# Gates' projection in seven half products with weight sets through a ring of three, and sums of halves of h on GpSimd

## The chip, the cores and the metric

One core of a Trainium2 chip. Its engines are named PE (TensorE's matmuls; PEld its weight loads), DVE (VectorE), ACT (ScalarE), POOL (GpSimd) and SP (SyncE, which here only issues DMAs). The metric is the device time of one execution in microseconds, the median of the runs.

## The reference, cut to what matters

One layer of a hybrid decoder on 4096 tokens of width 1024, in float32. All groups read one input h and come from one projection; each is multiplied by its own SiLU gate.

```
shift, scale, gate = jnp.split(c_act @ ada_w + ada_b, 3, axis=-1)
h = _rmsnorm(x, g_pre) * (1.0 + scale[:, None]) + shift[:, None]
proj = h @ w_in
aq, ak, av, ag, rkv, rg, gq, gkk, gv, gg = jnp.split(proj, ...)
attn = _sliding_window_attention(aq, ak, av, sinks) * jax.nn.silu(ag)
rwkv = _rwkv7_mixer(h, rr, rk, rv, ...) * jax.nn.silu(rg)
gla = _gla_mixer(h, gq, gkk, gv, ...) * jax.nn.silu(gg)
y = jnp.concatenate([attn, rwkv, gla], axis=-1) @ w_out
return x + gate[:, None] * _rmsnorm(y, g_post)
```

The gates' projection is the part of h @ w_in that gives ag, rg and gg: 1024 by 1024 weights for each token.

## The kernel before, in words

The tokens are cut into 16 pieces of 256 (NS = 16, NT = 256). Every large product is made of three matmuls in f16: each operand is split in a high and a low f16 part, and high x high, high x low and low x high are summed in PSUM.

*First half* (to about 980 us). For each piece, h is made and kept in DRAM (hscr), and the two recurrent mixers run; their results go to DRAM (mscr). In stage_c (line 949), which goes along with the pieces, the weights that the second half needs are read in f32, scaled, split in f16 parts and written to DRAM: seven sets of 256 columns of w_in (wscr), and the output weights. Those are cut in four quarters, and group (918) makes from the quarters the seven operands of a product by half blocks, with GpSimd for the differences (tile cs), ACT and VectorE for the splits (tile ch), into woscr.

*Second half*. One trip for each piece i (stage_p2, 1970): the output projection of piece i-1 (outp), the gates of piece i, and the projection of q, k and v for piece i+1 (qkv, heads_of). Beside these run the attention of a piece (stage_s, attend) and stage_m (1791), which multiplies the mixers' results (tiles mxa, mxb) by the gates (tile ag), finds a scale from their sum of squares (the small product mp, then tiles mtot to msc), and splits sums and differences of their halves into four f16 blocks (tile mtp, block at 1769).

- gates_of (1675): four products of 256 columns, tile gp, two PSUM banks (pj) in turn for all of gp, qp, kp and op. Weights q3 to q6 stay in SBUF for the whole half. Each product is two times 24 matmuls with 256 tokens moving, and is read twice: ACT's tanh and VectorE's multiplication. Two buffers of ag serve in turn, so gates(i) waits for the use of ag by piece i-2 ("og").
- outp (1867): seven products of a half block (tile op), 12 matmuls of 512 columns each. Weights of four products stay in SBUF (tiles o), three go through one buffer (ov), whose halves SP loads again when they have been used. VectorE adds each product to tile yv.
- heads_of (1625): kp (24 matmuls), two products qp (48 each), vp (48 of 128 columns). kp is read by ACT and VectorE into kT, two times two instructions each; qp into q.
- attend (1700): scores sc = q x k in eight groups of matmuls, read by a VectorE instruction with a maximum (CUSTOM in the profile), exponentials on ACT, the product with v (ovp).

The order is not that of the code. Every instruction is noted with a modelled cost (Order.note, 100), and pin (225) lays the instructions of each engine in a fixed row; an instruction of the row waits for its semaphores, and those behind it wait with it. PE, DVE, ACT, POOL and SP each have one such row.

All calls go through one helper, so in the profile nearly every instruction has line L339; the names of tiles tell them apart.

Of the kernel before, what the change touches and what calls it, by code (L numbers as in the profile page):

```python
# [35 lines left out]
URGENT = 150  # L36
HOME = {('kp', 'mq'): 'tr', ('cw', 'm'): 'at'}
# [366 lines left out]
def hybrid_kernel(ctx, tc, x, xc, rows, ada1, adaw, w1, wl, w2, wo, cst, abias, out):  # L404
# [45 lines left out]
    wscr = dp.tile([7, P, 2, KD * 256], F16, name="wscr")  # L450
# [180 lines left out]
    w_inv = [cp.tile([P, 1], F32, name=f"winv{n}") for n in range(8)]  # L631
    wo_ss = cp.tile([P, 2 * KD], F32, name="wo_ss")
    wo_sc = cp.tile([P, 1], F32, name="wo_sc")
    g_h = [cp.tile([P, 1], F32, name=f"gh{n}") for n in range(4)]
# [9 lines left out]
    with ExitStack() as p1:  # L644
# [264 lines left out]
        def wo_squares(h):  # L909

            for j in range(8 * h, 8 * h + 8):
                s32 = piece(wo, j * 512)
                yield [s32]
                square(s32, wo_ss[:, j : j + 1])
            if h:
                yield from total(wo_ss, wo_sc, w_inv[7])

        def group(k, c):

            left, right = [wt([P, 512], "cs", 2).rearrange("p (h n) -> p h n", h=2) for _ in range(2)]  # L920
            for t, k8 in ((left, k), (right, 4 + k)):
                for h in range(2):
                    at = (c + 2 * h) * 2048 + k8 * 256
                    SP.dma_start(t[:, h], wo[:, at : at + 256])
# [3 lines left out]
            def parts(t, p, m):  # L928
# [3 lines left out]
                S.activation(z[:, :, 0, :], t, AF.Identity, scale=wo_sc)  # L932
                V.scalar_tensor_tensor(z[:, :, 1, :], t, wo_sc, z[:, :, 0, :], op0=ALU.mult, op1=ALU.subtract)
                for n in range(m):
                    to = woscr[p + n, :, k, 2 * c : 2 * c + 2]
# [13 lines left out]
        def stage_c(i):  # L949

            yield [("c", i - 1), ("vg", i)]
            for n in ((0,), (1, 2), (3,), (4, 5), (6,))[i] if i < 5 else ():
# [31 lines left out]
                if n > 2:  # L984
                    V.tensor_single_scalar(g_h[n - 3], inv, 0.5, op=ALU.mult)
            if 4 <= i < 6:
                yield from wo_squares(i - 4)
            elif 6 <= i < NS - 2:
                yield from group((i - 6) % 4, (i - 6) // 4)
# [557 lines left out]
    def pool2(name):  # L1547
# [3 lines left out]
        "q", "kT", "vt", "w5", "w6", "ab", "v4", "pr", "pT", "mxa", "ag", "mtp", "mxb", "sm1", "o1", "o6", "o4", "o5", "ov")}  # L1551
# [8 lines left out]
    Wq = []  # L1560
# [6 lines left out]
    def stage_w(_):  # L1567

        load_h(0)
        order = (2, 0, 1, 3, 4, 5, 6)  # L1570
        got = {}
        for n in order:
            slot = wslot if n < 5 else lambda name: pools[f"w{name[1]}"].tile([P, KD, 256], F16, name=name)
            got[n] = load_2(n, slot(f"q{n}h"), slot(f"q{n}l"))
            if n == 1:
                load_h(1)
        Wq.extend(got[n] for n in range(7))
# [89 lines left out]

    def gates(i):
        yield [("og", i - 2)]
        f = F[i]  # L1670
        f["ag"] = ag = t_A([P, 8, NT], "ag") if i == 0 else pools["ag"].tile([P, 8, NT], F32, name="ag2") if i == 1 else F[i - 2]["ag"]
        yield from gates_of(f["hT"], ag, pjt)
        done.add(("gates", i))

    def gates_of(hT, ag, pj):

        for n in range(4):
            yield ["pj"]
            gp_ = pj("gp")
            for b in range(2):  # L1680
                yield from proj(gp_[:, b * NT : (b + 1) * NT], Wq[3 + n], b * P, P, hT)
            av = ag[:, 2 * n : 2 * n + 2, :].rearrange("p b n -> p (b n)")
            model.order.urgent = URGENT
            S.activation(av, gp_, AF.Tanh, scale=g_h[n])
            V.scalar_tensor_tensor(av, av, 1.0, gp_, op0=ALU.add, op1=ALU.mult)
            model.order.urgent = 0
# [91 lines left out]
    def mix_scale(mss):  # L1778
# [9 lines left out]
        V.tensor_mul(oi, miv, w_inv[7])  # L1788
        return msc, oi

    def stage_m(i):
# [45 lines left out]

    def load_o(t, n):
# [360 lines left out]
```

## Time and profile before

| | |
|---|---|
| median of 3 runs | 1996.33 us (1994.67 to 1996.79) |
| the profiled execution's own time | 1996.2 us |
| its span, first to last instruction | 1994.4 us |
| mean granted TensorE clock | 0.991 |
| busy: PE, PEld, DVE | 1882.8, 1453.4, 1427.5 us |
| busy: ACT, POOL | 1115.0, 373.1 us |
| DMA, mean | 129 GB/s |

A row of busy time counts what an engine executes; PE's matmuls overlap, so the time from one matmul's start to the next one's says more of the pace than the duration of one. In the rows of a tile, the three numbers are the shortest, the median and the longest duration in ns. In a timeline, the bracket at the end says how long the engine had been idle and for whom it waited.

### The profile page before, as it was taken

The numbers are of one execution on the slowest core, as the hardware profiler recorded it, in microseconds if no ns is written. First come the engines' busy times: TensorE is split into PE (matmuls) and PEld (weight loads), VectorE is DVE, ScalarE is ACT, GpSimd is POOL, SyncE is SP. The second block draws the span as 40 slices with busy tenths as digits, with TensorE's granted clock in tenths as the row PEclk, the third lists the DMA queues.
The fourth block names the chain that finished last, engine by engine and source line by source line (L and its number), as shares of the span: only waits on it lengthen the run. The fifth ranks groups of instructions, "written<-read, shape, count | busy, mean of one in ns | idle before, by whom it ended". The sixth has DMA issues, their size and how long they took to land.

```text
span 1994.4 us, 59065 instructions
## 1 busy us (share of the span) xinstructions
PE 1882.8 (94%) x24651; PEld 1453.4 (73%) x24651; DVE 1427.5 (72%) x3919; ACT 1115.0 (56%) x2529; POOL 373.1 (19%) x549
## 2 busy tenths in 40 slices
PE   5799989999999999999999999999999999999997
PEld 1677777777777777777776677876778767787793
DVE  4877877788877888777647776667666676666766
ACT  4877878677786676565435443344434444434443
POOL 0623223543223454223200000000000000000001
PEclk8999999999999999999999999999999999999999
DMA  9345544443342433125234433344333443334315
GB/s 373 128 152 179 155 140 125 148 139 109 105 133 88 125 111 111 61 65 185 77 132 142 151 109 112 109 146 130 109 110 109 149 130 109 100 117 151 110 47 181
DMA packets 154261, 257.55 MB, mean 129 GB/s; under 512 B 49026, under 2 KB 100994, under 8 KB 147844
## 3 DMA queue, kind: packets, MB, share of 16 engines
q1 hardware_dynamic: 153844, 253.19, 39.7%
q8 instruction: 195, 3.19, 0.7%
q14 instruction: 78, 0.64, 0.1%
q10 hardware_dynamic: 144, 0.52, 0.1%
HBM read 192.83 MB, written 60.82 MB: 127 GB/s over the span
## 4 chain that ended last, share of the span: by engine, by line
PE 55%; DVE 23%; DMA 9%; ACT 6%; issue 4%; POOL 1%; SPq 1%; ACTq 0%; DVEq 0%; POOLq 0%
PE gp L339 16%; PE op L339 11%; PE qp L339 5%; PE zz L339 4%; PE pv L339 2%; PE kp L339 2%; PE ovp L339 2%; PE lp L339 2%; DVE mtp L339 2%; DVE q L339 2%; PE sc L339 2%; DVE tsc L339 1%; SPq L339 1%; PE gqk L339 1%; DMA ov<-woscr 1%
## 5 line engine op out<-in xcount | busy, mean ns | idle before, releaser
L339 PEld LDWEIGHTS <-mtp 128*128 128x128 f16 x1344 | 128.7, 98 | 144.9 <-issue 9.2
L339 ACT ACTIVATE pr<-pr,nm,lsc 128x160 f32<-128x160 f32 (+2 forms) x256 | 129.0, 506 | 101.8 <-DVE nm L339 101.7
L339 PE MATMUL op<-o,mtp 128*128 128x512 f16 x768 | 182.2, 379 | 1.9 <-DVE yv L339 1.7
L339 PE MATMUL op<-ov,mtp 128*128 128x512 f16 x576 | 140.8, 379 | 4.4 <-DMA ov<-woscr 4.4
L339 PEld LDWEIGHTS <-hT 128*128 128x128 f16 x1536 | 117.6, 99 | 24.0 <-ACT hT L339 3.9
L339 ACT ACTIVATE ag<-gp,gh 128x512 f32<-128x512 f32 x64 | 43.9, 686 | 158.8 <-PE gp L339 158.8
L339 POOL TENSOR_TENSOR ry<-sy,expo 128x1 f32<-128x1 f32 x30 | 17.7, 606 | 584.7 <-DVE sy L339 584.7
L339 DVE SCALAR_TENSOR_TENSOR ag<-ag,gp 128x512 f32<-128x512 f32 x64 | 43.7, 683 | 103.1 <-ACT ag L339 103.1
L339 DVE TENSOR_TENSOR yv<-op,yv 128x512 f32<-128x512 f32 x105 | 72.1, 688 | 59.0 <-PE op L339 39.6
L339 PE MATMUL pv<-gvh,hT 128*128 128x272 f16 x512 | 98.2, 284 | 6.3 <-ACT hT L339 3.8
L339 PE MATMUL zz<-hT,kh 128*128 128x256 f16 x512 | 93.0, 274 | 0.0
L339 PE MATMUL zz<-hT,rh 128*128 128x256 f16 x512 | 92.5, 277 | 0.1
L339 PE MATMUL lp<-hT,Lh 128*128 128x256 f16 x512 | 91.7, 273 | 0.3 <-ACT vg L339 0.3
L339 PE MATMUL gqk<-hT,gqkh 128*128 128x256 f16 x512 | 87.9, 273 | 3.4 <-DVE zb L339 3.3
L339 DVE CUSTOM_DVE_ANT_0 pr<-sc,ab,kept 128x160 f32<-128x160 f32 (+2 forms) x256 | 83.1, 375 | 10.7 <-PE sc L339 10.2
L339 PE MATMUL gp<-hT,q4h 128*128 128x256 f16 x512 | 90.1, 276 | 0.0
L339 PE MATMUL qp<-hT,q1h 128*128 128x256 f16 x512 | 87.0, 275 | 0.9 <-DVE kT L339 0.9
L339 PE MATMUL qp<-hT,q0h 128*128 128x256 f16 x512 | 86.3, 273 | 0.5 <-issue 0.5
L339 PE MATMUL zz<-hT,vh 128*128 128x256 f16 x512 | 86.3, 273 | 0.0
L339 PE MATMUL gp<-hT,q3h 128*128 128x256 f16 x512 | 85.3, 273 | 0.0
L339 PE MATMUL gp<-hT,q5h 128*128 128x256 f16 x512 | 85.1, 273 | 0.0
L339 PE MATMUL gp<-hT,q6h 128*128 128x256 f16 x512 | 85.0, 273 | 0.0
(429 smaller groups left out, 5736.6 us busy)
## 6 DMA issues: line engine op xcount, KB each, us to landing
ov<-woscr SPq DMA_DIRECT2D x96, 512.0 KB, 4.5
xh<-in_x SPq DMA_DIRECT2D x32, 512.0 KB, 4.4
xt<-in_xc SPq DMA_DIRECT2D x16, 1024.0 KB, 8.2
hscr<-hT SPq DMA_DIRECT2D x16, 1024.0 KB, 5.0
hT<-hscr SPq DMA_DIRECT2D x16, 1024.0 KB, 5.0
x<-in_x SPq DMA_DIRECT2D x30, 512.0 KB, 4.2
out<-yv SPq DMA_DIRECT2D x30, 512.0 KB, 2.9
cs<-in_w SPq DMA_DIRECT2D x56, 256.0 KB, 3.6
```

The costliest lines, as they stand in the source:

```text
L339: r = f(*args, **kw)
```

## The change

The gates' weights are prepared like the output weights: one scale for all, quarters, seven operands by group, stored in wgscr. h of a piece is seen as two halves of tokens by two halves of channels. Three of the seven products take a quarter of h as it is; four take a sum of quarters, which half_sums makes: 10 additions and subtractions of 128x512 on POOL (tile sf), 4 copies to f16 on ACT and 4 more subtractions on POOL for the low parts (tile hs, one buffer). gates(i) then has seven products of 48 matmuls, each with 128 tokens moving and a weight load of its own. Products are added to ag in place by VectorE (seven additions and one copy by ACT for a piece); the four tanh (tile gt) and the multiplications that follow read SBUF. There is one buffer of ag, so gates(i) waits for the use by piece i-1. half_sums(i + 1) is issued behind gates(i).

Odd products' weights stay in SBUF (g1, g3, g5 for the gates, o1, o3, o5 for the output). Even products of both take their weights from a ring of three buffers (r0 to r2) in the order of use; as soon as a product has used its buffer, SP loads into it the set that is needed three sets later (next_set). A trip so loads eight sets of 1 MB in place of three.

PLAN says in which piece of the first half a group of weights is made: 0 to 7 are the gates', 8 to 15 the output's. Stages 0 and 1 do the three sets that are left of wscr, stages 2 and 3 the squares of the gates' weights.

The core of the diff:

```diff
+PLAN = {4: (0,), 5: (1,), 6: (2, 3), 7: (4, 5), 8: (6, 7), 9: (8, 9), 10: (10,), 11: (11, 12), 12: (13,), 13: (14, 15)}
...
-            for n in ((0,), (1, 2), (3,), (4, 5), (6,))[i] if i < 5 else ():
+            for n in ((0,), (1, 2))[i] if i < 2 else ():
...
+            for n in PLAN.get(i, ()):
+                src, first, scr, scale = ((w2, 3 * 2048, wgscr, wg_sc), (wo, 0, woscr, wo_sc))[n // 8]
+                yield from group(src, first, scr, scale, n % 4, n // 4 % 2)
...
+    def next_set():
+        n = next(sent)
+        if n < len(sets):
+            load_set(ring[n % 3], *sets[n])
...
+    def half_sums(i):
...
+        z, h = wt([P, 4, 2, 4, P], "hs", 1, F16), wt([P, 4, P], "sf", 1)
...
+        def parts(n):
+            S.activation(z[:, n, 0], h, AF.Identity)
+            G.tensor_tensor(z[:, n, 1], h, z[:, n, 0], op=ALU.subtract)
...
+        chain((h, hi[1][0], hi[1][1], add), (h, h, lo[1][0], add), (h, h, lo[1][1], add))
+        parts(0)
+        chain((h, h, hi[0][0], sub), (h, h, lo[0][0], sub))
+        parts(1)
+        chain((h, hi[0][1], h, sub), (h, h, lo[0][1], add))
+        parts(3)
+        chain((h, hi[0][0], hi[1][0], sub), (h, h, lo[0][0], add), (h, h, lo[1][0], sub))
+        parts(2)
+
     def gates(i):
-        yield [("og", i - 2)]
+        yield [("og", i - 1)]
...
+        def product(n):
+            yield ["pj"]
+            po = pjt("gp")
+            W, A = Wg[n] if n % 2 else ring[next(taken) % 3], given[n]
+            for k in range(KD // 2):
+                for m in range(4):
+                    for a, b in ((0, 0), (1, 0), (0, 1)):
+                        PE.matmul(po[:, m * P : m * P + P], W[k // 2][:, k % 2, m, a, :], A[:, b, k, :],
+                                  start=k == m == a == b == 0, stop=k == 3 and m == 3 and b == 1)
+                yield
+            if n % 2 == 0:
+                next_set()
...
+        def silu(c):
+            t = wt([P, 4, P], "gt", 1)
+            S.activation(t, c, AF.Tanh, scale=g_h)
+            V.scalar_tensor_tensor(c, t, 1.0, c, op0=ALU.add, op1=ALU.mult)
...
+        yield from product(4)
+        add(c22, c12)
+        add(c21, c21)
+        silu(c22)
+        yield from product(5)
+        add(c21, c21)
+        silu(c21)
+        yield from product(6)
+        add(c12, c12)
+        silu(c12)
         done.add(("gates", i))
...
-        for n in range(4):
-            yield ["pj"]
-            gp_ = pj("gp")
-            for b in range(2):
-                yield from proj(gp_[:, b * NT : (b + 1) * NT], Wq[3 + n], b * P, P, hT)
...
-            S.activation(av, gp_, AF.Tanh, scale=g_h[n])
-            V.scalar_tensor_tensor(av, av, 1.0, gp_, op0=ALU.add, op1=ALU.mult)
```

How it moves instructions in a trip. VectorE, from the end of the gates to mtot; ag is the gates, mxa and mxb the mixers' results, sm a sum of their halves. Before:

```order
L339 SCALAR_TENSOR_TENSOR ag<-ag,gp 128x512
L339 SCALAR_TENSOR_TENSOR mxb<-mxb,gh_103,ag 128x512
L339 SCALAR_TENSOR_TENSOR ag<-ag,gp 128x512
L339 SCALAR_TENSOR_TENSOR mxb<-mxb,gh_104,ag 128x512
L339 TENSOR_TENSOR sm_20922<-mxa,mxb 128x512
L339 TENSOR_TENSOR mxa<-mxa 128x4x128
L339 SCALAR_TENSOR_TENSOR kT<-kp,kq_s,kT 64x256 x4
L339 SCALAR_TENSOR_TENSOR q<-qp,q 64x8x64 x2
L339 TENSOR_REDUCE mtot<-mp 128x1
```

Now (the gates' tanh is in gt):

```order
L340 TENSOR_TENSOR ag<-gp,ag 128x4x128
L340 SCALAR_TENSOR_TENSOR mxa<-mxa,g_h,ag 128x512
L340 SCALAR_TENSOR_TENSOR ag<-gt,ag 128x4x128
L340 SCALAR_TENSOR_TENSOR mxb<-mxb,g_h,ag 128x512 x2
L340 SCALAR_TENSOR_TENSOR kT<-kp,kq_s,kT 64x256 x2
L340 TENSOR_TENSOR sm_29822<-mxa,mxb 128x512
L340 TENSOR_TENSOR mxa<-mxa 128x4x128
L340 SCALAR_TENSOR_TENSOR kT<-kp,kq_s,kT 64x256 x2
L340 SCALAR_TENSOR_TENSOR q<-qp,q 64x8x64 x2
L340 TENSOR_REDUCE mtot<-mp 128x1
```

An addition on gp and a multiplication of mxa have come in ahead of kT, both multiplications of mxb stand in a row, and the first pair of kT stands ahead of sm and mxa.

POOL, one trip and the start of the next (ry is the output norm's power, kT a copy of keys). Before:

```order
L339 COPY kT<-kT 128x4x128
L339 TENSOR_TENSOR ry<-sy,expo 128x1 x2
L339 COPY kT<-kT 128x4x128
L339 TENSOR_TENSOR ry<-sy,expo 128x1 x2
L339 COPY kT<-kT 128x4x128
L339 TENSOR_TENSOR ry<-sy,expo 128x1 x4
```

Now:

```order
L340 TENSOR_TENSOR ry<-sy,expo 128x1 x2
L340 TENSOR_TENSOR hs<-sf,hs 128x512
L340 TENSOR_TENSOR sf<-sf,hT 128x512 x2
L340 TENSOR_TENSOR hs<-sf,hs 128x512
L340 TENSOR_TENSOR sf<-hT,sf 128x512
L340 COPY kT<-kT 128x4x128
L340 TENSOR_TENSOR sf<-sf,hT 128x512
L340 TENSOR_TENSOR hs<-sf,hs 128x512
L340 TENSOR_TENSOR sf<-hT 128x512
L340 TENSOR_TENSOR sf<-sf,hT 128x512 x2
L340 TENSOR_TENSOR hs<-sf,hs 128x512
L340 TENSOR_TENSOR sf<-hT 128x512
```

Two rows of small work have become a row of fourteen sums a trip: the three first sums of a piece stand ahead of ry, eleven behind it, where the first (hs) waits for ACT's copy, which waits for the gates' last product.

ACT, from the gates' last tanh to the blocks' splits (mtp,mss are the sums of squares). Before:

```order
L339 ACTIVATE ag_17825<-gp,gh_104 128x512
L339 ACTIVATE mtp,mss<-mxb 128x1024
L339 ACTIVATE kT<-kp,kq_s 64x256 x4
L339 ACTIVATE q<-qp 64x8x64 x2
L339 ACTIVATE mtp<-mxa,msc 128x512
L339 ACTIVATE mtp<-mxb,msc 128x512
L339 ACTIVATE mtp<-sm_23295,msc 128x512
L339 ACTIVATE q<-qp 64x8x64
L339 ACTIVATE mtp<-mxa,msc 128x512
L339 ACTIVATE q<-qp 64x8x64
```

Now:

```order
L340 ACTIVATE hs<-sf 128x512
L340 ACTIVATE gt<-ag,g_h 128x512
L340 ACTIVATE mtp,mss<-mxa 128x1024
L340 ACTIVATE kT<-kp,kq_s 64x256 x2
L340 ACTIVATE mtp,mss<-mxb 128x1024
L340 ACTIVATE kT<-kp,kq_s 64x256 x2
L340 ACTIVATE hs<-sf 128x512
L340 ACTIVATE q<-qp 64x8x64 x2
L340 ACTIVATE hs<-sf 128x512
L340 ACTIVATE mtp<-mxa,msc 128x512
L340 ACTIVATE q<-qp 64x8x64
L340 ACTIVATE mtp<-mxb,msc 128x512
```

Three of the four copies to hs stand in this stretch; the second is ahead of the reads of qp, the third ahead of the first block's split.

On PE, mp stands behind 36 of the 48 matmuls of the second product qp; before, it ran behind 15 of them. The third group of sc stands behind five more matmuls of op than before.

More of the change, by code (lines that the diff above doesn't have):

```diff
@@ L907, in total, with squares, group @@
             pow2(sc, inv, tot)
-        def wo_squares(h):
+        def squares(src, at, ss, h):
             for j in range(8 * h, 8 * h + 8):
-                s32 = piece(wo, j * 512)
+                s32 = piece(src, at + j * 512)
                 yield [s32]
[L914 to L918, printed above, removed]
+                square(s32, ss[:, j : j + 1])
+        def group(src, first, scr, scale, k, c):
             left, right = [wt([P, 512], "cs", 2).rearrange("p (h n) -> p h n", h=2) for _ in range(2)]
@@ L1559, in hybrid_kernel, with set_tile, halves, load_set @@
     ab = pools["ab"].tile([P, 2, 160], BF16, name="ab")
-    Wq = []
+    Wq, Wg, ring = [], {}, []
+    OUTS = (0, 1, 6, 3, 4, 5, 2)
+    calls = [("g", 0), ("g", 1), ("o", 0), *((k, i + (k == "g")) for i in range(1, NS - 2) for k in "og"),
+             ("g", NS - 1), ("o", NS - 2), ("o", NS - 1)]
+    sets = []
+    for k, i in calls:
+        order = (1, 0, 2, 3, 4, 5, 6) if (k, i) == ("o", NS - 1) else range(7)
+        sets.extend((wgscr, OUTS[n]) if k == "g" else (woscr, OUTS[n]) for n in order if n % 2 == 0)
+    sent, taken = itertools.count(), itertools.count()
+    whole = []
+    def set_tile(name):
+        t = pools[name].tile([P, KD // 2, 4, 2, P], F16, name=name)
+        if name in ("r0", "r1"):
+            whole.append(t)
+        return t
+    def halves(tiles):
+        if len(tiles) == 1:
+            return [tiles[0][:, 2 * h : 2 * h + 2] for h in range(2)]
+        return [t.rearrange("p k c -> p (k c)").rearrange("p (k m b n) -> p k m b n", k=2, m=4, b=2) for t in tiles]
+    def load_set(t, scr, n, hs=(0, 1)):
+        for h in hs:
+            SP.dma_start(t[h], scr[n, :, 2 * h : 2 * h + 2])
+    def next_set():
+        n = next(sent)
+        if n < len(sets):
+            load_set(ring[n % 3], *sets[n])
     def load_2(n, h, l):
@@ new lines, in add @@
+        def add(to, z):
+            model.order.urgent = URGENT
+            V.tensor_tensor(to, f["pg"], z, op=ALU.add)
+            model.order.urgent = 0
+        def silu(c):
+            t = wt([P, 4, P], "gt", 1)
+            S.activation(t, c, AF.Tanh, scale=g_h)
+            V.scalar_tensor_tensor(c, t, 1.0, c, op0=ALU.add, op1=ALU.mult)
+        yield from product(0)
+        model.order.urgent = URGENT
+        S.copy(c21, f["pg"])
+        model.order.urgent = 0
+        yield from product(1)
@@ L1881, in product @@
             yield [f["blk"][n]]
-            A, (w, stays) = f["blk"][n], PRODUCTS[n]
-            W = Wr[w] if stays else Wv
+            A, m0 = f["blk"][n], n % 2 == 0
+            W = ring[next(taken) % 3] if m0 else Wr[n]
             for k in range(KD // 2):
                 for a, b in ((0, 0), (0, 1), (1, 0)):
-                    PE.matmul(po, A[:, a, k, :], W[:, k, :, b, :], start=k == a == b == 0,
+                    PE.matmul(po, A[:, a, k, :], W[k // 2][:, k % 2, :, b, :], start=k == a == b == 0,
                               stop=k == KD // 2 - 1 and a == 1)
-                if k == 1 and not stays:
-                    later = [m for m, s in PRODUCTS[n + 1 :] + PRODUCTS[: n + 1] if not s][0]
-                    if n < 6 or i < NS - 1:
-                        SP.dma_start(Wv[:, 0:2], woscr[later, :, 0:2])
-                if k == 3 and not stays and (n < 6 or i < NS - 1):
-                    SP.dma_start(Wv[:, 2:4], woscr[later, :, 2:4])
                 yield
+            if m0:
+                next_set()
             for m in ((4, 5), ())[n] if i == NS - 1 and n < 2 else (n + len(blocks),) if n + len(blocks) < 7 else ():
@@ L2100, in hybrid_kernel @@
                 SP.dma_start(fxt, wo[:, n * 2048 : (n + 1) * 2048])
[L2101 to L2103 removed]
+                split_f(wo_sc)
                 for a in range(2):
```

124 lines of the change are left out of this document (77 added, 47 removed).

## The prediction

> **What bounds the kernel now.** First the table of busy time by stage, cut where the second half begins and where its last trip starts (columns: window, its length, then busy us and instructions of PE, PEld, DVE, ACT and POOL, the granted clock, the DMA share, GB/s).
>
> ```profile
> 0.00:980.00 980.00, 905.89 (x13745) 713.64 (x13746) 764.53 (x2287) 682.85 (x1443) 337.61 (x494) 0.99 0.42 136
> ...
> 1060.00:1900.00 840.00, 819.73 (x9039) 618.21 (x9037) 556.79 (x1335) 360.44 (x906) 23.56 (x41) 1.00 0.40 124
> ```
>
> In the stretch from 1060 to 1900 us, all trips alike, PE is busy for 819.73 of 840 us at full clock, and POOL for 23.56 us. So a microsecond taken from PE's work is a microsecond of the kernel, provided that nobody makes PE wait. The waits of PE from 1060 us to the end say how close the others are (us in total, times, longest):
>
> ```profile
> PE sc L339 <- DVE q L339: 6.3, 25, 0.3
> ...
> PE op L339 <- DMA ov<-woscr: 4.4, 5, 2.1
> PE op L339 <- DVE yv L339: 1.7, 8, 0.6
> ...
> PE sc L339 <- DVE m L339: 1.1, 2, 1.0
> PE qp L339 <- DVE kT L339: 0.9, 1, 0.9
> ```
>
> Short, but the first comes twice in every trip: the scores' matmuls (sc) arrive just before VectorE is done with q. VectorE is therefore on time with nothing to spare at that place. Its timeline there, from the end of the gates (PE starts kp at 1401.06) on, in one trip:
>
> ```profile
> 1401.98 0.69 DVE L339 SCALAR_TENSOR_TENSOR ag<-ag,gp 128x512 f32<-128x512 f32 x1 [3.77 <-ACT ag L339]
> 1402.71 0.75 DVE L339 SCALAR_TENSOR_TENSOR mxb<-mxb,gh,ag 128x512 f32<-128x512 f32 x1
> ...
> 1405.51 0.97 DVE L339 SCALAR_TENSOR_TENSOR kT<-kp,kq_s,kT 64x256 f16<-64x256 f32 x2 [0.61 <-ACT kT L339]
> 1407.50 0.99 DVE L339 SCALAR_TENSOR_TENSOR kT<-kp,kq_s,kT 64x256 f16<-64x256 f32 x2 [1.02 <-ACT kT L339]
> ...
> 1411.81 0.16 DVE L339 TENSOR_REDUCE mtot<-mp 128x1 f32<-128x2 f32 x1
> ...
> 1413.82 0.75 DVE L339 SCALAR_TENSOR_TENSOR mtp<-mxa,msc,mtp 128x512 f16<-128x512 f32 x1 [0.53 <-ACT mtp L339]
> ...
> 1418.94 0.75 DVE L339 SCALAR_TENSOR_TENSOR mtp<-sm,msc,mtp 128x512 f16<-128x512 f32 x1
> 1419.71 0.38 DVE L339 CUSTOM_DVE_ANT_0 pr<-sc,ab,kept 128x160 f32<-128x160 f32 x1
> ```
>
> From mtot at 1411.81 to the first read of the scores at 1419.71 there is one gap, of 0.53 us. This stretch of some 19 us is where the change puts its GpSimd work.
>
> **PE: eight half products become seven.** PE's timeline at the end of the gates (256 columns) and in the values' projection (vp, 128 columns, a weight load ahead of each matmul, as the new product has it):
>
> ```profile
> 1399.64 0.27 PE L339 MATMUL gp<-hT,q6l 128*128 128x256 f16 x1
> ...
> 1400.95 0.27 PE L339 MATMUL gp<-hT,q6l 128*128 128x256 f16 x1
> 1401.06 0.38 PE L339 MATMUL kp<-hT,q2h 128*128 128x256 f16 x2
> ```
> ```profile
> 1416.20 0.22 PE L339 MATMUL vp<-q2l,hT 128*128 128x128 f16 x1
> ...
> 1416.87 0.22 PE L339 MATMUL vp<-q2l,hT 128*128 128x128 f16 x1
> ```
>
> q6l comes once in three matmuls, so 12 take 1400.95 - 1399.64 = 1.31 us, 0.109 each. q2l also, so 12 take 0.67 us, 0.056 each. A set of gates has 4 x 2 x 24 = 192 matmuls of the first kind, 21.0 us; the seven products have 7 x 48 = 336 of the second, 18.8 us. That saves 2.2 us in each of 16 sets: **-35.5 us**. It is less than an eighth of 21.0 because a matmul of 128 columns takes a little over half of one with 256.
>
> **GpSimd: what its sums do to VectorE.** A set of sums is 14 operations on 128x512. The nearest rows of POOL (tiles gaw and kT), and VectorE's and POOL's timelines at a place where both are busy:
>
> ```profile
> L339 POOL TENSOR_TENSOR gaw<-gaw,scol x16: 1035/1040/2018, 48.9 to 410.9; 128x512 f32<-128x512 f32 x16
> ...
> L339 POOL COPY kT<-kT x15: 609/609/611, 954.9 to 1847.4; 128x512 f16<-128x512 f16 x15
> ```
> ```profile
> 49.37 1.70 DVE L339 SCALAR_TENSOR_TENSOR kl<-stgRA,wsc,kh 128x1024 f16<-128x1024 f32 x1 [0.84 <-ACT kh L339]
> 50.99 1.52 DVE L339 TENSOR_TENSOR hT<-xt,hT 128x512 f16<-128x512 f32 x1
> 52.44 1.74 DVE L339 SCALAR_TENSOR_TENSOR kl<-stg,wsc,kh 128x1024 f16<-128x1024 f32 x1
> ```
> ```profile
> 48.95 3.02 POOL L339 TENSOR_TENSOR gaw<-gaw,scol 128x512 f32<-128x512 f32 x2 [10.18 <-DMA gaw<-in_adaw]
> 51.93 2.84 POOL L339 TENSOR_TENSOR gaw<-gaw 128x256 f32<-128x256 f32 x2
> ```
>
> No row shows a sum of f16 tensors on POOL. It lies between the copy of f16, which reads one tensor (0.61 us), and the sum of f32, which reads two (1.04); I take 1.04, for the two reads: 14.6 us a set.
>
> Two of gaw's operations of 1.04 took 3.02 us, and VectorE's subtraction in hT took 1.52. They ran in turns: kl ends at 51.07, the second gaw at 51.97, the subtraction at 52.51. So one GpSimd operation that gets in between holds VectorE back by 51.97 - 51.07 = 0.90 us. Which VectorE operations this meets, the spread of their durations says (min/median/max):
>
> ```profile
> L339 DVE SCALAR_TENSOR_TENSOR ch<-cs,wo_sc,ch x32: 452/745/1548, 642.1 to 782.2; 128x512 f16<-128x512 f32 x24, 128x256 f16<-128x256 f32 x8
> ...
> L339 DVE TENSOR_TENSOR AT<-atp,masks x64: 659/680/693, 101.2 to 951.6; 128x512 f32<-128x512 f32 x64
> ...
> L339 DVE SCALAR_TENSOR_TENSOR zb<-zz,mu_c,zs x96: 459/475/488, 71.2 to 933.2; 128x256 f32<-128x256 f32 x96
> ...
> L339 DVE SCALAR_TENSOR_TENSOR mtp<-sm,msc,mtp x16: 744/751/752, 1062.9 to 1967.0; 128x512 f16<-128x512 f32 x16
> ```
>
> ch has both tensors in SBUF and went up to 1548 ns in the first half, where POOL is busy a third of the time. AT and zb read one tensor from PSUM (atp, zz), and 160 of them in the same half never went over 693 and 488. mtp is of ch's kind and never over 752, in the half where POOL idles. So in the second half the multiplications by the gates, the blocks' splits and differences will be held; the readings of kp, qp and sc will not, but stand in the queue behind them. The Trainium skill says the same (SBUF — State Buffer, Who interferes with whom: a VectorE instruction with two SBUF inputs and a GpSimd instruction that reads SBUF take a shared port in turn, and the later one blocks for the whole of it); the 0.90 agrees, and with that rule it speaks against this change.
>
> Now the places, counted along the order of the changed kernel. *First, kp's bank.* qp's second product needs the PSUM bank that the last kT frees. That was at 1407.50 + 0.99 = 1408.49; that product comes after kp's 24 and the first query product's 48 matmuls of 256 columns, at 1401.06 + 72 x 0.109 = 1408.9: 0.4 us spare. In the new order four operations of the held kind (mxa, ag, mxb twice) stand ahead of kT, with the addition on the gates' last product, and three GpSimd operations (the first difference, two sums) are ready then: 3 x 0.90 = 2.7 us. The two gaps of 0.61 and 1.02 us ahead of kT take most of the added VectorE work (0.69 + 0.75) and the spare some of the rest. I take a PE stall of **1.8 us**, between 0 and 2.7. *Second, the scores.* In the new order, between mp and the first reading of sc, VectorE has seven held operations (oi, four splits, two differences), and 8 of the 14 GpSimd operations are left, so about four get in: 3.6 us. The third sc now stands behind 5 more matmuls of op, but mp stands 21 matmuls later in its product, so the spare is at most 0.7: **2.9 us**, between 1 and 4.5. Of the sum 0.5 replaces the two waits for q that PE has already: 4.2 us for a trip, in the 13 trips that have this order, **+54.6 us** (2 to 6.5 a trip: 26 to 84). ACT's four copies for a set go in its gaps (it is busy for 360.44 of 840 us), but each waits for POOL, and behind the third of them on ACT stands the first split: what POOL loses to VectorE comes back there, which is within the upper bound.
>
> **The rest.** (a) First half: 16 groups instead of 8, and 3 sets instead of 7, so 8 more splits of 512 columns and 8 of 256 on DVE and ACT each, 10 us by the ch rows' medians, and 32 more sums on POOL. PE covers it, being busy 905.89 of 980 us; if each microsecond came through it were 10; I take **+4**. (b) At the start the sums for the first set need 14 x 1.04 us and four copies, about 17 us, under kp, qp and vp (120 x 0.109 + 48 x 0.056 = 15.8 us) and two products of 2.7 that use no sums; but POOL still has the first half's tail then. 0 to 6, I take **+2**. (c) The waits for ov of 4.4 us go: a ring slot has at least four products (each 6144 columns, 2.7 us), 10.8 us, from its last use to its next, and by
>
> ```profile
> ov<-woscr SPq DMA_DIRECT2D x96, 512.0 KB, 4.5
> ```
>
> each half lands 4.5 us after its issue. Eight sets of 1 MB a trip stand where three stood, in SP's one queue, between out, x, hT and v; I take **-3** (-4.4 to 0; its bad end is a rival). (d) VectorE's 7 additions on gp for a set, 0.69 each, and ACT's one copy read PSUM like the yv additions and lie under products of 2.7 us with two banks; the trace shows 1.7 us of waits for yv in all; nothing. (e) Gates now wait for the previous trip's use of ag, not the one before that; the output product ahead of them needs it anyway, and in the last trip a projection of 15.8 us covers it; nothing.
>
> The profiled execution took 1996.2 us, 0.1 under the median of the runs. Sum: 1996.2 - 35.5 + 54.6 + 4 + 2 - 3 = **2018 us**.
>
> **The rivals.**
> *VectorE takes the turns in its gaps (faster).* For it: from 1060 to 1900 it is idle for 283 us, and in the first half 764.53 us of DVE and 337.61 of POOL go along with PE at 92%. Against it: the gaps are under gates and output, the sums under the projection. If no stall comes, 1996.2 - 35.5 + 3 = 1964 us; the sign turns where a trip's stall passes 32.5 / 13 = 2.5 us. Chance 0.36.
> *Weight loads bind.* The loads on 128 columns have their own row:
>
> ```profile
> L339 PEld LDWEIGHTS <-hT 128*128 128x128 f16 x1536 | 117.6, 99 | 24.0 <-ACT hT L339 3.9 <-issue 3.2 <-DVE kg L339 1.0
> ```
>
> Were they not overlapped, 336 x 0.099 = 33.3 us for a set instead of 21.0, +196: 2190 us. The vp rows with 0.056 speak against it. Chance 0.03. The Trainium skill has a milder form (TensorE: Matmul & The Clock Gate, Back-to-back issue gap: about 81 ns sustained for 128 columns with a load each); an estimate by it is 27.2 us for a set, 99 us more in all. The vp rows disagree with it.
> *The ring comes late.* Eight sets a trip in one queue, in order: if each made PE wait 1 us in 13 trips, 104 us, 1996.2 - 35.5 + 104 = 2065 without the stall. Ten microseconds of lead against 4.5 speak against it. Chance 0.05.
>
> **How the numbers follow.** The forecast's chance is 0.56, its own range with 2 to 6.5 us of stall 1990 to 2048. A measurement here tells 0.2%, 4 us, from no change. Faster: the first rival, less its top, 0.35; within 4 us: the seam between it and the forecast, 0.08; slower: the rest, 0.57. The range 1966 to 2047 leaves out the bottom of the first rival (0.08) and the top of the forecast with the last two rivals (0.12).
>
> **What would show it.** Right: gp matmuls 0.056 apart; POOL busy about 630 us; the rows of mxb, mtp and the mxa differences with a maximum of 1.5 us or more; PE's wait for kT about 20 us in all, and its waits for q and m together some 40. Wrong: those rows still under 0.8 us, or a span under 1985. A wait of gp or op for the DMA of the ring over 10 us would be the third rival.

## The result, and the profile after

After, the kernel takes 2093.02 us (median of 4 runs, 2081.53 to 2100.79); before, beside it on the same chip, 1996.56 (1994.67 to 1998.09). The ratio is 1.048, 95% interval 1.042 to 1.054: slower by 96 us, 75 us more than forecast and past the top of the range. The profiled execution took 2098.5 us (span 2096.6).

The table of busy time by stage, with the same cuts and columns as before:

```profile
0.00:980.00 980.00, 908.15 (x13782) 717.24 (x13783) 777.64 (x2270) 690.15 (x1461) 361.60 (x527) 0.98 0.43 139
980.00:1060.00 80.00, 58.97 (x1033) 50.41 (x1030) 37.00 (x117) 27.18 (x74) 42.24 (x39) 0.85 0.45 151
1060.00:1900.00 840.00, 745.43 (x9864) 581.83 (x9862) 643.38 (x1329) 372.55 (x895) 243.34 (x204) 0.97 0.55 188
```

The first half is as it was. From 1060 to 1900 PE is busy for 745 us instead of 820, and the granted clock is 0.97 instead of 1.00. POOL has gone from 24 to 243 us, the DMA from 124 to 188 GB/s. From 980 to 1060, where the second half starts, PE is busy for 59 us and its granted clock is 0.85; before, it was

```profile
980.00:1060.00 80.00, 75.92 (x1123) 65.32 (x1120) 46.46 (x161) 34.17 (x95) 5.97 (x8) 1.00 0.37 124
```

Four rows place the loss: the first mp of the second half comes late, and the trips between two mp are longer (tile mp, then PE's timeline at the third and the fourteenth mp, of before and of after).

```profile
L339 PE MATMUL mp<-mss,first x32: 168/214/251, 1049.7 to 1948.1; 128*128 128x2 f32 x32
```
```profile
1160.57 0.17 PE L339 MATMUL mp<-mss,first 128*128 128x2 f32 x1
...
1849.27 0.17 PE L339 MATMUL mp<-mss,first 128*128 128x2 f32 x1
```
```profile
L340 PE MATMUL mp<-mss,first x32: 168/251/272, 1068.6 to 2063.6; 128*128 128x2 f32 x32
```
```profile
1195.85 0.28 PE L340 MATMUL mp<-mss,first 128*128 128x2 f32 x2
...
1945.29 0.28 PE L340 MATMUL mp<-mss,first 128*128 128x2 f32 x2
```

The start costs 1068.6 - 1049.7 = 18.9 us (forecast: 6 for first half and start together). Eleven trips take 749.4 instead of 688.7: 68.13 each instead of 62.61, 5.5 more where I had some 1.8. PE's waits from 1060 us to the end:

```profile
PE sc L340 <- DVE m L340: 31.6, 15, 2.4
PE qp L340 <- DVE kT L340: 25.9, 14, 2.0
PE ovp L340 <- issue: 17.3, 9, 2.9
PE sc L340 <- DVE q L340: 14.1, 12, 1.2
PE op L340 <- DVE mtp L340: 7.1, 12, 0.6
PE gp L340 <- issue: 4.9, 4, 1.7
```

Before, the rows of m, kT and q had 1.1, 0.9 and 6.3. The two places of the prediction are there, at nearly its size: kT 25.9 us (forecast about 20), q and m together 45.7 (some 40). VectorE's timeline through one trip, from the end of the gates to the first read of the scores, shows the holds themselves:

```profile
1388.66 1.61 DVE L340 SCALAR_TENSOR_TENSOR mxa<-mxa,g_h,ag 128x512 f32<-128x512 f32 x1
1390.20 1.64 DVE L340 SCALAR_TENSOR_TENSOR ag<-gt,ag 128x512 f32<-128x512 f32 x1
1391.87 2.19 DVE L340 SCALAR_TENSOR_TENSOR mxb<-mxb,g_h,ag 128x512 f32<-128x512 f32 x2
...
1403.04 1.13 DVE L340 TENSOR_TENSOR oi<-miv,winv 128x1 f32<-128x1 f32 x1
...
1406.32 1.64 DVE L340 SCALAR_TENSOR_TENSOR mtp<-mxb,msc,mtp 128x512 f16<-128x512 f32 x1
...
1408.71 1.14 DVE L340 TENSOR_TENSOR mxb<-mxb,mxa 128x512 f32<-128x512 f32 x1
1409.78 1.64 DVE L340 SCALAR_TENSOR_TENSOR mtp<-mxa,msc,mtp 128x512 f16<-128x512 f32 x1
1411.34 1.64 DVE L340 SCALAR_TENSOR_TENSOR mtp<-sm,msc,mtp 128x512 f16<-128x512 f32 x1
1412.99 0.39 DVE L340 CUSTOM_DVE_ANT_0 pr<-sc,ab,kept 128x160 f32<-128x160 f32 x1
```

Eight operations are held (one of the two mxb in the pair), each by 0.45 to 0.96 us; all read two tensors in SBUF. Over the eleven trips, VectorE's operations that took over 0.15 us longer than the median of their kind without GpSimd work add up to 6.6 us a trip. I call this sum **held** below. What GpSimd's operations take themselves (tiles sf and hs, 1100 to 1980 us; min/median/max):

```profile
L340 POOL TENSOR_TENSOR sf<-sf,hT x87: 1154/1482/1623, 1100.0 to 1956.4; 128x512 f32<-128x512 f32 x87
...
L340 POOL TENSOR_TENSOR hs<-sf,hs x49: 1153/1156/1162, 1102.4 to 1952.0; 128x512 f16<-128x512 f32 x49
```

1.15 us where nothing holds them, 1.48 in turns; I had taken 1.04. POOL is busy for 688.2 us in all, not 630.

What I had not priced stands in two other places. The stops for nothing that the profile shows (issue: ovp and gp) grew from 5.9 + 1.6 to 17.3 + 4.9 us. And after some stops TensorE is slow for a while. The granted clock just behind a stop of 2.4 us that ends at 1343.32, and PE's timeline, one matmul of 512 columns within that while and one behind it:

```profile
1344.20:1347.60 3.40, 3.40 (x16) 1.75 (x14) 2.52 (x14) 1.29 (x4) 0.00 (x0) 0.50 0.32 114
```
```profile
1346.60 0.63 PE L340 MATMUL op<-o,mtp 128*128 128x512 f16 x1
...
1347.83 0.38 PE L340 MATMUL op<-r,mtp 128*128 128x512 f16 x1
```

Comparing every start of a matmul with the usual spacing of its kind, the eleven trips split as follows: usual spacing 631.4 us (before: 657.7), single stops over 0.3 us 93.1 (21.2), the rest, mostly slow matmuls, 24.8 (9.8).

### The profile page after: what moved, and what is told of

It reads as the page before. It is cut to its first block, busy times and chain, and to the rows that moved or that the text cites. A ratio compares the mean times of both kernels' runs of the same rounds, so it can differ in the third digit from the quotient of the medians.

```text
span 2096.6 us, 64661 instructions
## 1 busy us (share of the span) xinstructions
PE 1883.2 (90%) x26949; PEld 1478.3 (71%) x26949; DVE 1603.0 (76%) x4013; ACT 1173.2 (56%) x2625; POOL 688.2 (33%) x805
## 4 chain that ended last, share of the span: by engine, by line
PE 46%; DVE 30%; DMA 7%; ACT 7%; issue 6%; SPq 2%; POOL 2%; DVEq 0%; ACTq 0%; POOLq 0%
PE gp L340 12%; PE op L340 11%; PE zz L340 4%; PE qp L340 4%; DVE mtp L340 4%; DVE ag L340 3%; SPq L340 2%; PE ovp L340 2%; DVE mxa L340 2%; PE pv L340 2%; PE sc L340 1%; DVE ch L340 1%; DMA cs<-in_w 1%; PE gqk L340 1%; DVE tsc L340 1%
## 5 line engine op out<-in xcount | busy, mean ns | idle before, releaser
L340 PE MATMUL op<-r,mtp 128*128 128x512 f16 x768 | 187.7, 383 | 9.2 <-DVE mtp L340 7.1
L340 POOL TENSOR_TENSOR hs<-sf,hs 128x512 f16<-128x512 f32 x64 | 74.1, 1158 | 366.1 <-ACT hs L340 366.1
L340 PEld LDWEIGHTS <-r 128*128 128x128 f16 x3072 | 181.2, 100 | 17.7 <-DMA r<-wgscr 7.0
L340 POOL TENSOR_TENSOR sf<-sf,hT 128x512 f32<-128x512 f32 x112 | 158.6, 1416 | 7.8
L340 PE MATMUL gp<-hs,r 128*128 128x128 f16 x2304 | 148.3, 224 | 12.5 <-DMA r<-wgscr 6.4
L340 PEld LDWEIGHTS <-g 128*128 128x128 f16 x2304 | 139.9, 102 | 5.4 <-issue 4.4
L340 ACT ACTIVATE gt<-ag,g_h 128x512 f32<-128x512 f32 x64 | 46.2, 721 | 163.7 <-DVE ag L340 163.7
L340 DVE TENSOR_TENSOR ag<-gp,ag 128x512 f32<-128x512 f32 x112 | 75.1, 683 | 79.8 <-PE gp L340 79.8
L340 PE MATMUL qp<-hT,q1h 128*128 128x256 f16 x512 | 89.9, 280 | 25.9 <-DVE kT L340 25.9
L340 PE MATMUL sc<-kT,q 128*128 128x160 f16 (+2 forms) x512 | 57.6, 239 | 45.7 <-DVE m L340 31.6
L340 PE MATMUL gp<-hT,g 128*128 128x128 f16 x1536 | 92.0, 219 | 2.0 <-issue 1.5
```

Of the source, the lines that this page charges most:

```text
L340: r = f(*args, **kw)
```

## The experiments

Fifteen kernels; each ratio is to the kernel before on the same chip, with its 95% interval. Worked out from the traces, one execution each: the start of the first mp, the mean of the eleven trips from the third to the fourteenth mp, and what VectorE is held in one.

| kernel | us | ratio | first mp | trip | held |
|---|---|---|---|---|---|
| before | 1996.56 | 1 | 1049.7 | 62.61 | 0 |
| after | 2093.02 | 1.048 [1.042, 1.054] | 1068.6 | 68.13 | 6.6 |
| no_sums | 2002.57 | 1.003 [1.001, 1.005] | 1073.1 | 61.10 | 0 |
| memsets | 2004.76 | 1.005 [1.002, 1.008] | 1070.4 | 61.58 | 0 |
| before_sums | 2052.03 | 1.028 [1.025, 1.031] | 1064.7 | 64.89 | 3.0 |
| no_sums_no_ring | 1985.79 | 0.994 [0.991, 0.996] | 1068.7 | 60.15 | 0 |
| ring_twice | 2097.33 | 1.050 [1.047, 1.054] | 1075.0 | 67.06 | 0 |
| early_r2 | 2098.43 | 1.050 [1.048, 1.052] | 1079.8 | 68.16 | 6.7 |
| early_r2_no_sums | 2001.94 | 1.003 [1.001, 1.005] | 1072.3 | 60.94 | 0 |
| r2_moved | 1992.30 | 0.997 [0.996, 0.998] | 1062.8 | 61.62 | 0 |
| r2_moved_no_sums | 1990.45 | 0.997 [0.995, 0.999] | 1061.7 | 61.24 | 0 |
| late_sums | 2058.74 | 1.032 [1.028, 1.036] | 1069.5 | 64.93 | 3.5 |
| late_o3 | 2113.64 | 1.060 [1.057, 1.063] | 1071.8 | 69.37 | 5.1 |
| late_o3_pool | 2052.19 | 1.027 [1.024, 1.029] | 1061.0 | 65.41 | 6.0 |
| late_o2_pool | 2065.31 | 1.035 [1.032, 1.037] | 1060.0 | 66.57 | 7.1 |
| pool_copies | 2091.45 | 1.048 [1.046, 1.050] | 1064.6 | 68.29 | 7.4 |
| dve_sums | 2102.77 | 1.051 [1.048, 1.054] | 1064.8 | 69.50 | - |

### What do the sums cost, and by what?

**no_sums** leaves half_sums out for all sets but the first:

```diff
         f = F[i]
+        if i > 0:
+            f["hs"] = F[0]["hs"]
+            return
```

> Leaves out the 14 sums and 4 copies of every set but the first (the later gates read the first set's sums, so their values are not the reference's). Seven products, the ring and the new order stay. Theory (GpSimd's sums hold VectorE's operations on two SBUF tensors, TensorE stops for those, and runs its matmuls slower for some us after a stop): in 11 trips TensorE's stops and slow matmuls are 117.9 us after and 31.0 before, 7.9 a trip more; without the sums these go, 13 x 7.9 = 103 us, and some 10 of the 24 us lost at the start of the second half: 2093 - 113 = 1980 us, between 1965 and 1995, with no VectorE row of mxb or mtp over 0.8 us. Rival (the 85 MB more of weight sets in SP's queue, and what else the ring brings): 2070 or more. Rival (the new order and the one buffer of ag): 2050 or more.

**memsets** keeps the chain but takes GpSimd's reads away:

```diff
-            G.tensor_tensor(z[:, n, 1], h, z[:, n, 0], op=ALU.subtract)
+            G.memset(z[:, n, 1], 0.0)
...
-                G.tensor_tensor(to, a, b, op=op)
+                G.memset(to, 0.0)
```

(The planner is told 1.19 us for such a memset, as for a sum.)

> Each of the 14 sums becomes a memset of the same tile on GpSimd, which reads no SBUF; the four copies of ACT, the waits between the engines and the planned order stay (the gates' products with sums are not the reference's). Theory (what holds VectorE is GpSimd reading SBUF): near the kernel without sums, 1985 us, between 1965 and 2005, VectorE's rows of mxb and mtp at their short durations. Rival (it is not the reading but the waits of the chain GpSimd, ACT, GpSimd and the order planned around it): 2060 or more.

**before_sums** puts half_sums, with its calls, into the kernel before; its outputs go to two small tiles that nothing reads.

> The kernel before, whose gates stay eight half products, does the same 14 sums and 4 copies for each set into tiles that nothing reads. Theory: VectorE's held operations cost 4.6 us of its time a trip (60 us in the rows of mxa, mxb, mtp and ag after), TensorE's stops and slow matmuls 7.9: 1996 + 60 to 103 = 2056 to 2099, say 2080. Rival (ring or new order): nothing reads the sums, 1996 to 2010.

Measured: 2002.57, 2004.76 and 2052.03 us. Without the sums 2093.0 - 2002.6 = **90 us** go, and nearly all of it without GpSimd's reads alone: the memsets leave 2 us of it. VectorE's splits, tile mtp, in that run from 1195 to 1900 us, and GpSimd's memsets:

```profile
L340 DVE SCALAR_TENSOR_TENSOR mtp<-mxb,msc,mtp x35: 744/747/751, 1195.4 to 1883.0; 128x512 f16<-128x512 f32 x35
```
```profile
L340 POOL MEMSET sf<- x110: 524/524/527, 1233.7 to 1860.3; 128x512 f32 x110
```

They write the same tiles and hold nobody: no split over 752 ns, against some 1640 after. The Trainium skill says so (SBUF — State Buffer, Who interferes with whom: the contention is with a GpSimd instruction that reads SBUF, not with one that only writes it); this run agrees. That the memsets are also half as long as the sums leaves a small doubt, but held is zero, not half. The waits between GpSimd and ACT, which are shorter here, and the new order are then not the main cause. One wait of PE stays in memsets, though nothing is held there:

```profile
PE op L340 <- DVE mtp L340: 7.1, 12, 0.6
```

After, this wait is 5.9 us in the same stretch; no_sums doesn't list it, nor does pool_copies below, which has no copies of hs on ACT. So some 0.5 us a trip comes from those copies or from the order laid out with them; which of the two isn't shown.

before_sums adds 55 us and lands just under the expected range (2056 to 2099): in the old order other operations are met, and VectorE is held for 3.0 us a trip. The trip grows by 2.3, PE's waits in it (1195 to 1900 us) stand at the scores, and the first mp comes 15 us later:

```profile
PE sc L339 <- DVE q L339: 20.4, 22, 2.1
PE sc L339 <- DVE m L339: 7.0, 9, 0.8
```

The forecast for no_sums failed, though: 2003 is not 1980. Where the sums are gone, the kernel is still no faster than before. Something else eats the gain.

### What eats the gain of the matmuls?

**no_sums_no_ring** also stops the ring's loads after the ninth (`if n < len(sets)` becomes `if n < 9`). **ring_twice** is no_sums with each load of the ring issued twice.

> Leaves out all sums but the first set's, and all loads of sets into the ring after the ninth (the products read old sets). Without sums a trip takes 61.10 us against 62.61 before, 0.85 short of the 2.35 that the matmuls save; TensorE stops 0.65 more at the values' product ovp, for nothing that the profile shows, and 0.45 in the gates. Theory (the loads hold up TensorE's instructions): 60.3 us a trip, 2003 - 11 = 1992, between 1988 and 1997, the start unchanged. Rival (it is the order or the many small matmuls): 2000 or more.

> Without all sums but the first set's; each load of a set into the ring is issued twice, so that the traffic of the ring doubles (8 MB more a trip). The loads cost 0.95 us a trip (61.10 with, 60.15 without). Theory (their traffic slows what else moves, TensorE's instructions among it): 1 us a trip more, 2003 + 17 = 2020, between 2010 and 2032, with more stops of TensorE at ovp for nothing that the profile shows. Rival (it is the place of the loads in SP's queue): the second loads land 3 to 5 us later than the first, so TensorE waits for the ring: 2040 or more. Rival (neither): 2003.

Measured: 1985.79 and 2097.33 us; the first is a little under its range (1988 to 1997). The loads that the ring needs cost 2002.6 - 1985.8 = **17 us**, 0.95 a trip. (The four kernels with the ring and without these sums scatter from 60.94 to 61.62 a trip, so the 0.95 may be 0.8 to 1.5.) PE's waits from 1195 to 1900 us, with the loads (no_sums) and without:

```profile
PE ovp L340 <- issue: 12.2, 10, 1.8
PE gp L340 <- issue: 4.1, 5, 1.3
```
```profile
PE ovp L340 <- issue: 6.5, 6, 1.5
...
PE gp L340 <- issue: 2.6, 2, 1.6
```

No wait for a ring load is among them. The loads cost in stops that have no releaser in the profile, 16.3 against 9.1 us; the rest is in shorter stops and slow matmuls.

The trace's transfers show what ends these stops. The page of no_sums has, among the queues (packets, MB):

```profile
q8 instruction: 213, 3.49, 0.7%
```

A packet is 16 KB. TensorE's 26949 matmuls and 26949 weight loads, divided by 213, are 253 to a packet; before, 2 x 24651 by 195 are also 253. So queue 8 brings TensorE's instructions. In the eleven trips, every stop without releaser of over 0.5 us between two matmuls of one product gp or ovp ends 1.2 to 1.6 us after such a packet has landed: 5 of 5 before, 10 of 10 after, 13 of 13 in no_sums, 7 of 7 in no_sums_no_ring. These are waits for instructions, and the change itself brings more of them: 70 packets in eleven trips instead of 58. Why more of them come late beside the ring's loads stays open: a packet takes as long with the loads as without (median 0.96 and 0.97 us).

With each load issued twice the time grows by another 95 us, and now both kinds of stop appear:

```profile
PE gp L340 <- DMA r<-wgscr: 20.7, 10, 2.9
PE ovp L340 <- issue: 19.5, 7, 3.7
PE gp L340 <- issue: 9.5, 4, 4.3
```

So my expectation of 2020 fell, and its two cases aren't told apart: the second load of each set lands later, which makes the waits for r, and the stops without releaser nearly double too (29.0 against 16.3 us). Without sums and loads a trip takes 60.15 us, 2.46 under before. I take this as the gain of seven products, but it is counted without any loads, where before loads three sets a trip (from 1060 to 1900 the DMA moves 77 GB/s there, 124 before); so only the 2.46 and the 0.95 together compare the two kernels.

### What is lost at the start?

The first mp comes 10 to 30 us late in all kernels with the ring. PE's waits of after there (930 to 1075 us):

```profile
PE yt L340 <- POOL ysb L340: 10.3, 2, 6.2
PE gp L340 <- DMA r<-wgscr: 6.4, 1, 6.4
```

**early_r2** and **early_r2_no_sums** move r2, the ring's third tile, and g5 to other memory by the order of the pools; **r2_moved** and **r2_moved_no_sums** do it another way, without the sums (the last with none at all, a memset of hs in their place):

```diff
-        ... "mxa", "hs", "r2", "g5", "sf", "gt", "mtp", "mxb", "sm1", "o1", "o3", "o5")}
+        ... "mxa", "hs", "mtp", "mxb", "sm1", "gt", "sf", "r2", "g5", "o1", "o3", "o5")}
```

> The ring's third tile and the set g5 change places in SBUF with mtp, mxb and sm1, nothing else. In the kernel after and in the one without sums the first mp of the second half comes 19 and 23 us later than before, with or without sums; TensorE waits 6.4 us there for a load of the ring's third tile, which stands behind ysb, the last store of the first half. Theory (that memory comes free last, so the gates can't fill the tail of the first half): the wait and what follows go, 8 to 15 us: 2093 - 12 = 2081, between 2073 and 2087, first mp at 1050 to 1060. Rival (GpSimd's and ACT's chain, or the queue itself, holds the gates at the start): 2090 or more.

> The same exchange in the kernel that leaves out all sums but the first set's (later gates read the first set's sums). Theory: 2003 - 12 = 1991, between 1983 and 1996. Rival (the start is held by something else): 1999 or more. If the seven products are worth 2.35 us a trip and nothing else costs, 1996 - 35 = 1961 would be reached; I expect 30 us short of it.

> Without all sums but the first set's. In the earlier run with r2 and g5 moved, sf moved too, to memory that the first half frees late (GpSimd waited 19 us for PE yp), so it decided nothing. Now r2 and g5 move and sf stays. Theory (ring's third tile in late memory): the wait of 6 us for its load goes and the first mp comes at 1057 to 1066 instead of 1073; 2003 - 12 = 1991, between 1983 and 1997. Rival (the start is lost to the chain of the first set's sums): 2000 or more.

> The same with no sums at all (one memset in their place, so all products of sums read zeros). Theory of the ring's tile alone: the same as the run beside it within 3 us. Rival (the first set's sums hold the gates at the start): 8 us or more faster than the run beside it, 1975 to 1985. If neither moves the first mp from 1073, the start is lost to something else: 2000.

Measured: 2098.43, 2001.94, 1992.30 and 1990.45 us. The first pair lands on its rivals. It moved sf as well, into memory that the first half frees late (in the run without sums POOL waited 19.2 us for PE yp ahead of the first sum), so it doesn't tell what r2 alone is worth. In the second pair the wait for r is gone and the first mp comes at 1062.8 and 1061.7 instead of 1073.1: about **10 us** of the start are the place of r2, and the whole time falls by as much (2002.57 to 1992.30). After issues the second half of r2's load at 1024.47, right behind the store of ysb at 1024.08, the last of the first half. The first set's sums are worth 1 to 2 us there, within the spread of the runs. The other 12 us come from neither. The start of r2_moved_no_sums:

```profile
980.00:1060.00 80.00, 72.58 (x1207) 65.02 (x1208) 41.95 (x145) 28.72 (x76) 6.90 (x9) 0.87 0.55 172
```

Its granted clock is 0.87 where before has 1.00. That is worth up to 0.13 x 80 = 10 us, so most of the 12 can be TensorE's slow clock. Which of the stops there starts it isn't shown.

### Can the sums lie elsewhere?

**late_sums** starts a set's sums after the first output product, **late_o3** after the fourth, each by a copy that waits for that product:

```diff
+        if after is not None:
+            G.tensor_copy(h[:, 0, 0:1], after[:, 0:1])
```

**pool_copies** has `G.tensor_copy(z[:, n, 0], h)` in place of ACT's copy. **late_o3_pool** and **late_o2_pool** join this with r2 moved and the sums after the fourth or the third output product. **dve_sums** does all sums with V instead of G, ranked last.

> The same sums of the set for the next trip start only when the first output product of the trip has been copied (a GpSimd copy of one column of it stands ahead), so they lie under the output products and the first two gate products, where VectorE mostly reads PSUM, and not under the projection and the scores. All sets but three (the first three and the last keep their place or nearly). Theory: most of the 7.9 us a trip go; held there are the late splits, the norm and the softmax, so I keep 2 of 7.9: 2093 - 13 x 5.9 = 2016 us, between 1985 and 2050. Rival (ring or new order): 2080 to 2100, as after.

> As the run with late sums, but the sums of the next set start when the fourth output product of the trip has been added (GpSimd first copies a column of it), some 11 us later. In that run VectorE's held operations were 25 of 44 multiplications pr by rd, 11 splits mtp and 7 of 22 small sums, 3.2 us a trip, and a trip took 64.9 us; without sums 61.1. Theory (only holds in front of something TensorE needs soon cost): the first softmax and the splits are past by then, and what is left to hold is the norm, the gates' own products and half of the softmax; a trip of 62.5 us, 2059 - 13 x 2.4 = 2028, between 2005 and 2045. Rival (the holds cost wherever they fall, or the sums now come late for the gates): 2055 or more.

> The four copies of a set's sums go from ACT to GpSimd, nothing else. Held operations on VectorE make 4.35 us a trip after, slower matmuls 1.0 more than without sums, but the sums cost 7.0 a trip. Theory (the rest, some 1.6, is ACT waiting for GpSimd with the splits behind it in its queue): 2093 - 13 x 1.6 = 2072, less what four more GpSimd operations hold, 0 to 3 times 0.9 a trip: between 2065 and 2100, ACT's row of hs gone and its waits for sf with it. Rival (the rest is VectorE's queue alone, ACT is no part): 2093 or more, up to 2130.

> Sums after the fourth output product, their four copies on GpSimd instead of ACT, and the ring's third tile moved. In the run with the copies on ACT a trip took 69.4 us, of which the gates' stops for late sums were 5.3 and the gates' slow matmuls after them some 2.1, though VectorE was held for 5.1. Theory (a hold costs only where TensorE is about to need VectorE): both go, a trip of 62.0 to 63.0 us; 2114 - 13 x 6.9 - 10 = 2014, between 2000 and 2030. Rival (holds cost one for one wherever they fall): 61.1 + 5 to 6 = 66 to 67 a trip, 2060 to 2080.

> The same one output product earlier, so that the sums have 2.7 us more until the gates need them, and meet more of the softmax of the trip. Theory: held near the second half's pr by rd and the splits, 0.5 to 1.5 us a trip more than the run beside it unless that still waits for its sums: 2010 to 2040. Rival (one for one): 2060 to 2080, as the run beside it.

> VectorE does the 14 sums, ranked behind all its other work (the planner knows what they take, as it doesn't know that GpSimd holds VectorE), with the exchange of the ring's third tile. 14 x 0.69 = 9.7 us a trip on VectorE, which idles 840 - 625 = 215 us of 13.7 trips without sums, 15.7 a trip. Theory (what cost was GpSimd holding VectorE at unplanned places): a trip near 62.6 us, 1991 + 13 x 1.5 = 2010, between 1992 and 2035. Rival (VectorE becomes the bound, the gaps lie in the wrong places): trips of 65 us or more, 2040 or more.

Measured: 2058.74, 2113.64, 2091.45, 2052.19, 2065.31 and 2102.77 us. late_sums takes 34 us off, not the expected 77: the trip falls to 64.9 with 3.5 us held, over half of it the softmax's pr by rd. late_o3 is slower than after, for a reason of its own. ACT's copy of hs stands behind eight exponentials in its queue, GpSimd waits for it, and the gates wait for GpSimd:

```profile
1434.88 1.71 POOL L340 TENSOR_TENSOR hs<-sf,hs 128x512 f16<-128x512 f32 x1 [5.29 <-ACT hs L340]
```
```profile
PE gp L340 <- ACT hs L340: 46.7, 10, 5.6
PE op L340 <- DVE yv L340: 12.4, 10, 1.2
```

pool_copies leaves the time as it was, but it doesn't decide on ACT. The wait for mtp at op is gone with the copies, and in its place VectorE is held for 7.4 us a trip instead of 6.6, as GpSimd has four operations more; PE's waits lie elsewhere:

```profile
PE qp L340 <- DVE kT L340: 33.5, 10, 3.4
PE sc L340 <- DVE q L340: 30.6, 21, 2.3
```

So what ACT costs after can hide behind the added holds. The 1.6 us a trip that I expected for it isn't seen, and isn't refuted. In late_o3_pool the gates' wait shrinks to what GpSimd itself is late:

```profile
PE gp L340 <- POOL hs L340: 18.7, 20, 1.6
PE op L340 <- DVE yv L340: 17.7, 11, 1.6
```

It lands at 2052, between the theory (2000 to 2030) and its rival (2060 to 2080): 6.0 us are held, the trip is 4.3 over no_sums, and of that some 1.7 is the wait for hs (18.7 us in 11 trips). So there a held microsecond costs some 0.4 by this count; after, 7.0 us a trip for 6.6 held, it costs about one, slow matmuls included. late_o2_pool lands on its rival: its trip is 5.5 over no_sums, with 7.1 held, so some 0.8. Placement helps, but no place was free of cost. dve_sums takes GpSimd out and lands on its rival too, with 14 sums at 0.69 us on VectorE and a trip of 69.5. PE waits 31.5 us for m and q from 1195 to 1900, so VectorE is late for the scores; but stops without releaser are 29.7 us there, and the granted clock from 1060 to 1900 is 0.95 against 1.00 in no_sums. That VectorE alone is the bound isn't shown, and the run also has the places of early_r2. No version with the sums beats the kernel before.

## Why the prediction was wrong

The direction was right, and so was the main mechanism: GpSimd's reads hold VectorE, and TensorE waits behind it. Three terms of the sum failed. The sum was "1996.2 - 35.5 + 54.6 + 4 + 2 - 3 = 2018". Term by term, measured between kernels:

| term | forecast | measured | from |
|---|---|---|---|
| seven products | -35.5 | -32 | 13 trips of 62.61 - 60.15 |
| first half and start | +6 | +19 | first mp 1068.7 (no_sums_no_ring) less 1049.7 |
| ring, waits for ov | -3 | +17 | no_sums less no_sums_no_ring |
| GpSimd's sums | +54.6 | +90 | after less no_sums |
| together | +22 | +94 | the result: +96 |

**The matmuls: right.** PE's timeline in a gate product, 48 matmuls from one start to the next:

```profile
1382.24 2.84 PE L340 MATMUL gp<-hT,g 128*128 128x128 f16 x48
1384.92 0.78 PE L340 MATMUL gp<-hs,r 128*128 128x128 f16 x11
```

2.68 / 48 = 0.056 us, as taken from vp; weight loads don't bind. The usual spacing fell by 657.7 - 631.4 = 26.3 us in eleven trips, 2.4 each, where 2.2 were forecast; the -32 in the table has a little else in it, such as before's waits for ov.

**The holds: counted right, their time too low.** Expected were three held operations ahead of kT and four ahead of the scores, 0.90 each, 6.3 us; held are three and five, 6.6. At "First, kp's bank" PE waits 1.84 us a trip (20.2 in eleven), against 1.8. At "Second, the scores" it is 39.2 / 11 = 3.6, 3.0 over before, against 2.9 less 0.5. So gaps and spare time took some 1.8 us of the 6.6 held, about as I had let them (2.1), and the two places cost 4.8 where I had "4.2 us for a trip". But the sums cost 68.13 - 61.10 = 7.0 us a trip. The step that failed is that the term ended at those two waits and gave nothing to what else the sums bring. One part is the wait for mtp at op (5.9 us in ten trips, 0.6 each), which memsets has without holds. Another is slow matmuls after the stops: spacing beyond the usual is 24.8 us after and 13.6 in no_sums, 1.0 a trip. Some 0.6 a trip I can't place. That 7.0 comes out near the 6.6 held is chance.

**The ring: wrong in sign.** Step (c) compared the 10.8 us of lead with a landing time of 4.5 and saw no wait. In the trips there is none, and the waits for ov went as forecast. But the loads cost 17 us in stops without releaser and slow matmuls. The profile of before had such stops already (5.9 and 1.6 us), and I did not ask what makes them grow. The third rival's size, 1 us a trip, was right by luck: its sign, a wait for the DMA, came once at the start (6.4 us) and never in a trip.

**The start: too small.** Step (b) priced the first set's sums, 1 to 2 us in the end, and put nothing down for two other things: a ring tile that lies in memory freed last (some 10 us), and TensorE's slow clock there (up to 10). Step (a), +4 for the first half, isn't seen: the last kp of the first half starts at 962.9, before at 967.8, so the start itself loses 24 us.

**POOL's operation:** 1.04 was low, 1.15 to 1.48 is measured. It moved the sum little: the loss of one held operation was 0.90 by the forecast, and 6.6 / 8 = 0.83 on average.

The first rival, gaps that take the turns, is refuted for this order: PE's waits at kT and at the scores came to 4.8 us a trip over before. The range failed because its top was built from the holds alone (6.5 us a trip) and the three other terms were each given a few microseconds.

## What to carry to other kernels

Work on GpSimd that reads SBUF is paid in VectorE's queue: count the VectorE operations with two SBUF tensors that it will meet, and take each hold as lost unless the trace shows a gap right behind it and in front of the engine that waits (here 4.8 of 6.6 us came through). Add something for slow matmuls after the stops, 1.0 us a trip here. A saving that brings several megabytes more traffic into a loop can have a price even where every transfer lands in time; look whether the profile has stops without releaser, compare them with the instruction packets, and price them by a run without the loads. When a tile is added to SBUF, ask whose memory it takes and when that comes free.

## What the runs showed of the hardware

- What a held operation loses doesn't go by its own length: oi on 128x1 took 1.13 us instead of 0.16, a split on 128x512 1.64 instead of 0.75.
- A stop of 1.7 to 2.9 us can be followed by some 3.4 us in which TensorE's matmuls start at half the rate (gp 0.11 us apart instead of 0.056, the 0.63 us row above). After the same stop of 2.4 us at m it came in 4 of 11 trips, after the stop of 1.8 us at kT in none. The Trainium skill has the half rate and a window of about 3.4 us that runs freely (TensorE: Matmul & The Clock Gate, Part 1: The HAM clock gate); the half rate and the 3.4 us agree, and 4 of 11 fits a window that runs freely; but the page's table warns of gaps over about 3 us, and here shorter ones were enough.
- TensorE stops for its own instructions: all 35 stops counted above ended 1.2 to 1.6 us after a 16 KB packet of queue 8 had landed, one for some 253 instructions. The change brings 70 such packets in eleven trips instead of 58.
- The cost of the ring's loads grew faster than their bytes: 17 us for the loads, 95 more for the same loads again, though the second ones also land later.
